# Layer 0 weight split in a float32 decoder trunk: the low part written by ScalarE and an accumulating GpSimd transfer

## The chip, the cores and the metric

The kernel runs on one core of a Trainium2 chip. The metric is the device time of one execution in microseconds. A core has five engines with a queue of their own, each running its instructions in the order in which they stand: TensorE (PE, with its weight loads shown apart as PEld), VectorE (DVE), ScalarE (ACT), GpSimd (POOL) and SyncE (SP), which issues nearly all transfers here.

## The reference

A two-layer decoder trunk over 1024 tokens of width 1024, all in float32. Layer 0 mixes time with RWKV-7 and layer 1 with differential attention; each is followed by a gated convolutional feed-forward part.

```
for l in range(DEPTH):
    h = modulate(rms_norm(x, norm1[l]), sh1, sc1)
    if l < N_A:
        y, v_first = rwkv7_time_mix(h, ...)   # r, k, v = xr @ w_rkv[0], xk @ w_rkv[1], xv @ w_rkv[2]; ... (o * g) @ w_o
    else:
        y = diff_attention(h, k_sh, v_sh, ...)
    x = x + g1 * y
    h2 = modulate(rms_norm(x, norm2[l]), sh2, sc2)
    x = x + g2 * conv_glu_ffn(h2, ...)        # u = h2 @ w_up, a convolution over 3 tokens, silu(gate) * val, @ w_down
return rms_norm(x, final_norm)
```

## The kernel before, in words

A float32 product is made of three float32r products. A weight block W is split into a high part (W rounded to float32r) and a low part (W minus the high part), the activations likewise, and `mm3` (lines 107 to 111) multiplies high by high (L109), low weights by high activations (L110) and high by low (L111), all into one PSUM bank.

In layer 0 the weights of three products go through `mm_cols` (lines 156 to 169). One call makes one block of 128 output columns from pieces of 512 x 128 weights, 256 KB each. For a piece, SP loads it into a `wraw` buffer (L161), ACT rounds it into the high half of a `whl` buffer (L163), an engine that `low()` names subtracts and writes the low half (L164), and PE runs 4 times the three matmuls. With the constants at the end of the file (`LD = 1`, `LN = 0`) `low()` always names DVE. There are 232 pieces: 96 of `a_w_rkv` (48 for each half of the tokens), 48 of `a_w_o` and 88 of `ffn_w_up`. The `wraw` and `whl` buffers are few: 4 and 3 for the first half of `a_w_rkv`, 2 and 2 for its second half and for `a_w_o`, 2 and 4 for `ffn_w_up` (constants `WRB`, `WHB`, `FWR`, `FWH`; `out_proj` asks for 2 and 2).

Five stages use `mm_cols`, in this order:

- A: r, k, v of the first 512 tokens (`tm_proj(0)`), 48 pieces
- B: r, k, v of the other 512 tokens (`tm_proj(1)`), 48 pieces, woven with the recurrence
- C: the output projection of the first 512 tokens in two calls of 256 tokens (`out_proj`), 32 pieces whose matmuls have 256 columns, woven with the recurrence
- D: the feed-forward up product of the first 512 tokens (`ffn_pre`), 88 pieces, woven with the recurrence
- E: the output projection of the last 512 tokens, 16 pieces, alone

The recurrence (`wkv`) goes over eight tiles of 128 tokens, each a chain of small matmuls, DVE and ACT steps; POOL raises to the power -0.5 for it (L581, L307). After stage E the rest of layer 0's feed-forward part and layer 1 do not use `mm_cols`: their weights are split by `split` and `split_w` on ACT and DVE.

`weave`, `merge` and the loop in `trunk` say in which order pieces of work are emitted. A scheduler then places the instructions on each engine's queue; it moves an instruction ahead of others that it does not depend on, so that the rounding of a piece can stand in ACT's queue ahead of work on earlier pieces.

Of the kernel before, what the change touches and what calls it, by code (L numbers as in the profile page):

```python
# [9 lines left out]
F32 = mybir.dt.float32  # L10
F32R = mybir.dt.float32r
BF16 = mybir.dt.bfloat16
AF = mybir.ActivationFunctionType
ALU = mybir.AluOpType
# [3 lines left out]
P = 128  # L18
# [3 lines left out]
HS = 512  # L22
# [63 lines left out]
class Trunk:  # L86
# [69 lines left out]
    def mm_cols(self, ps, w, j, xh, xl, wraw, whl, khs=(0, 1)):  # L156

        nc = self.nc
        for i, kh in enumerate(khs):
            raw = wraw.tile([P, 4, P], F32, tag="wraw", name="wraw")  # L160
            nc.sync.dma_start(raw, w[kh * HS:(kh + 1) * HS, j * P:(j + 1) * P].rearrange("(k p) f -> p k f", p=P))  # L161
            wt = whl.tile([P, 2, 4, P], F32R, tag="whl", name="whl")
            nc.scalar.copy(wt[:, 0], raw)  # L163
            self.low().tensor_tensor(out=wt[:, 1], in0=raw, in1=wt[:, 0].bitcast(F32), op=ALU.subtract)  # L164
            for k in range(4):
                kk = 4 * i + k
                self.mm3(ps, wt[:, 0, k, :], wt[:, 1, k, :], xh[:, kk, :], xl[:, kk, :], kk == 0, kk == 4 * len(khs) - 1)
            if i + 1 < len(khs):
                yield
# [1691 lines left out]
```

## Time and profile before

| | |
|---|---|
| median of 3 runs | 3306.48 us (3298.51 to 3312.58) |
| the profiled execution's own time | 3304.96 us |
| its span on the core | 3303.2 us |
| mean granted TensorE clock | 0.943 of full speed |
| busy: PE, PEld, DVE, ACT, POOL | 91%, 73%, 65%, 37%, 3% of the span |
| stages A to E | about 109 to 1313 us of the span |

The profile is of one execution. A row of the groups by line gives the busy time of all instructions of one line and shape, the mean of one in ns, and the idle time of the engine right before them with what ended it. A timeline row is one instruction with its start and length; in brackets stands how long its engine had been idle and what it had waited for. In the table of windows a time of an engine is its busy time in that stretch, and PEclk is the granted share of the full clock.

### The profile page before, as it was taken

To read this page: it belongs to the slowest core of one execution; us is meant where nothing else is said; L and a number is where in the kernel's file an instruction comes from. 1 tells how busy PE (TensorE), PEld (TensorE's weight loads), DVE (VectorE), ACT (ScalarE), POOL (GpSimd) and SP (SyncE) were. 2 spreads that over 40 slices of the span, in tenths; PEclk is the share of its full clock that TensorE was granted. 3 is DMA by queue.
4 is the path that set the end of the run, shared out by engine and by line. 5 is a ranking of instruction groups with operands and counts; after the bars stand their busy time and mean duration, and the time that the engine had idled before them with its cause. 6 is when DMAs were issued, how large, how long until landed. Compare 5 with 4: busy or idle time off the path is not lost.

```text
span 3303.2 us, 53483 instructions
## 1 busy us (share of the span) xinstructions
PE 3004.2 (91%) x21607; PEld 2419.4 (73%) x21607; DVE 2152.5 (65%) x3752; ACT 1228.2 (37%) x2165; POOL 84.1 (3%) x50
## 2 busy tenths in 40 slices
PE   5988888987899997899999889898889999999997
PEld 2574667776677775788888678787678888888885
DVE  2656778566777855687777676777656655555555
ACT  3634455554454543322223333444333221222123
POOL 0000000000000000000000000000000000000000
PEclk7999899988899998999999899899899999999998
DMA  7363344343433337454443445445552111111111
GB/s 244 113 201 111 98 125 122 115 116 109 117 116 106 100 105 241 153 159 138 141 153 121 149 134 141 136 124 153 151 177 97 52 51 39 58 45 51 39 45 51
DMA packets 441402, 387.85 MB, mean 117 GB/s; under 512 B 42832, under 2 KB 369856, under 8 KB 440130
## 3 DMA queue, kind: packets, MB, share of 16 engines
q1 hardware_dynamic: 438850, 380.23, 38.3%
q8 instruction: 170, 2.79, 0.4%
q10 hardware_dynamic: 2304, 4.20, 0.3%
q14 instruction: 78, 0.64, 0.1%
HBM read 298.74 MB, written 83.49 MB: 116 GB/s over the span
## 4 chain that ended last, share of the span: by engine, by line
PE 68%; DVE 14%; DMA 6%; issue 6%; ACT 4%; POOL 1%; SPq 0%; DVEq 0%; POOLq 0%; ACTq 0%
PE u L109 9%; PE u L110 8%; PE u L111 8%; PE d L109 5%; PE d L111 5%; PE d L110 5%; PE ps L109 5%; PE ps L110 4%; PE ps L111 4%; DMA agw<-in_ada_w_dram 2%; PE wp L696 1%; PE sc L1539 1%; PE cp L745 1%; DVE AS L636 1%; PE tp L1466 1%
## 5 line engine op out<-in xcount | busy, mean ns | idle before, releaser
L109 PE MATMUL u<-h,whl 128*128 128x512 f32 x1408 | 561.8, 399 | 12.7 <-DVE mu L1089 10.0
L110 PE MATMUL u<-h,whl 128*128 128x512 f32 x1408 | 554.3, 394 | 6.2 <-DVE whl L164 6.2
L111 PE MATMUL u<-h,whl 128*128 128x512 f32 x1408 | 552.7, 393 | 0.0
L1134 DVE SCALAR_TENSOR_TENSOR x<-d,mod,x 128x512 f32<-128x512 f32 x352 | 261.8, 749 | 180.7 <-PE d L111 180.6
L109 PEld LDWEIGHTS u<-h,whl 128*128 128x128 f32 x1408 | 265.7, 189 | 73.5 <-ACT h L1090 10.2
L110 PEld LDWEIGHTS u<-h,whl 128*128 128x128 f32 x1408 | 265.8, 189 | 63.3 <-DVE whl L164 8.7
L111 PEld LDWEIGHTS u<-h,whl 128*128 128x128 f32 x1408 | 265.6, 189 | 59.6
L100 ACT CAST whl<-raw 128x1024 fp32r<-128x1024 f32 x140 | 143.9, 1042 | 433.6 <-PE d L111 421.5
L1046 DVE SCALAR_TENSOR_TENSOR a<-u,cwc,a 128x511 f32<-128x511 f32 (+1 forms) x132 | 122.0, 924 | 258.7 <-ACT a L1045 258.6
L109 PE MATMUL d<-hid,whl 128*128 128x512 f32 x704 | 280.1, 398 | 8.3 <-ACT hid L100 6.0
L110 PE MATMUL d<-hid,whl 128*128 128x512 f32 x704 | 277.3, 394 | 0.0
L111 PE MATMUL d<-hid,whl 128*128 128x512 f32 x704 | 275.4, 394 | 0.0
L1045 ACT ACTIVATE a<-u,cwc 128x512 f32<-128x512 f32 (+1 forms) x132 | 121.5, 921 | 390.9 <-PE u L111 390.5
L164 DVE TENSOR_TENSOR whl<-wraw,whl 128x512 fp32r<-128x512 f32 x232 | 158.0, 685 | 123.5 <-ACT whl L163 121.1
L163 ACT CAST whl<-wraw 128x512 fp32r<-128x512 f32 x232 | 142.7, 618 | 248.5 <-PE ps L111 102.9
L109 PE MATMUL ps<-xh,whl 128*128 128x512 f32 x384 | 162.7, 424 | 9.8 <-ACT xh L100 8.2
L101 DVE TENSOR_TENSOR whl<-raw,whl 128x1024 fp32r<-128x1024 f32 x140 | 168.9, 1217 | 4.0 <-ACT whl L100 3.8
L109 PEld LDWEIGHTS d<-hid,whl 128*128 128x128 f32 x704 | 133.2, 189 | 44.4 <-ACT hid L100 9.3
L111 PE MATMUL ps<-xl,whl 128*128 128x512 f32 x384 | 156.7, 409 | 4.6 <-DVE xl L101 4.3
L110 PE MATMUL ps<-xh,whl 128*128 128x512 f32 x384 | 156.4, 408 | 4.4 <-DVE whl L164 4.4
L111 PEld LDWEIGHTS d<-hid,whl 128*128 128x128 f32 x704 | 133.2, 189 | 30.3 <-DVE hid L101 1.6
L110 PEld LDWEIGHTS d<-hid,whl 128*128 128x128 f32 x704 | 133.3, 189 | 26.8
(279 smaller groups left out, 5863.9 us busy)
## 6 DMA issues: line engine op xcount, KB each, us to landing
raw<-in_ffn_w_up_dram SPq DMA_DIRECT2D x88, 512.0 KB
wraw<-in_a_w_rkv_dram SPq DMA_DIRECT2D x96, 256.0 KB
agw<-in_ada_w_dram SPq DMA_DIRECT2D x96, 256.0 KB
wraw<-in_ffn_w_up_dram SPq DMA_DIRECT2D x88, 256.0 KB
raw<-in_ffn_w_down_dram SPq DMA_DIRECT2D x44, 512.0 KB
agw<-in_ada_w_dram SPq DMA_DIRECT2D x128, 128.0 KB
rkv_d<-st SPq DMA_DIRECT2D x48, 256.0 KB
wraw<-in_a_w_o_dram SPq DMA_DIRECT2D x48, 256.0 KB
```

The source lines that it names most:

```text
L100: nc.scalar.copy(h, src)
L101: nc.vector.tensor_tensor(out=l, in0=src, in1=h.bitcast(F32), op=ALU.subtract)
L109: nc.tensor.matmul(ps, wh, xh, start=first, stop=False)
L110: nc.tensor.matmul(ps, wl, xh, start=False, stop=False)
L111: nc.tensor.matmul(ps, wh, xl, start=False, stop=last)
L163: nc.scalar.copy(wt[:, 0], raw)
L164: self.low().tensor_tensor(out=wt[:, 1], in0=raw, in1=wt[:, 0].bitcast(F32), op=ALU.subtract)
L636: nc.vector.tensor_tensor(out=AS[o, hh, :, c, :], in0=Av[o], in1=cst[o, W_AM:W_AM + 64].unsqueeze(1).to_broadcast([64, NK, 64]), op=ALU.mult)
L696: nc.tensor.matmul(Kp[o, j * 64:(j + 1) * 64], T.KB[r, j, c, :], KD[r, hh, c, j, :], start=True, stop=True)
L1045: nc.scalar.activation(a, u, AF.Identity, bias=c[3], scale=c[2])
L1046: nc.vector.scalar_tensor_tensor(out=a[:, 1:], in0=u[:, :n - 1], scalar=c[1], in1=a[:, 1:], op0=ALU.mult, op1=ALU.add)
L1134: nc.vector.scalar_tensor_tensor(out=xs, in0=ps, scalar=gate[:, j:j + 1], in1=xs, op0=ALU.mult, op1=ALU.add)
```

## The change

ACT writes the negated high part into the low half of the `whl` buffer, and a transfer issued by POOL reads the same 256 KB of weights from HBM again and adds them to that half in place. DVE's subtraction is gone. SP's load and ACT's rounding stay.

```diff
         for i, kh in enumerate(khs):
             raw = wraw.tile([P, 4, P], F32, tag="wraw", name="wraw")
-            nc.sync.dma_start(raw, w[kh * HS:(kh + 1) * HS, j * P:(j + 1) * P].rearrange("(k p) f -> p k f", p=P))
+            src = w[kh * HS:(kh + 1) * HS, j * P:(j + 1) * P].rearrange("(k p) f -> p k f", p=P)
+            nc.sync.dma_start(raw, src)
             wt = whl.tile([P, 2, 4, P], F32R, tag="whl", name="whl")
             nc.scalar.copy(wt[:, 0], raw)
-            self.low().tensor_tensor(out=wt[:, 1], in0=raw, in1=wt[:, 0].bitcast(F32), op=ALU.subtract)
+
+            nc.scalar.activation(wt[:, 1], wt[:, 0].bitcast(F32), AF.Copy, scale=-1.0)
+            nc.gpsimd.dma_start(wt[:, 1], src, accum_op=ALU.add)
```

Lines below this place have numbers higher by 3 in the changed kernel. The scheduler's order, at two places. First ACT's queue at the end of stage E (`sq` is the square of an output block, which waits for DVE, and DVE for that block's matmuls; the names in brackets are the semaphores an instruction waits on). Before:

```order
L849 ACTIVATE sq<-xs 128x512 [waits DVE_49,Activation_49]
L163 CAST whl<-wraw 128x512 [waits DMAHW3_49,PE_49,Activation_49]
L163 CAST whl<-wraw 128x512 [waits DMAHW7_49,DVE_49,PE_49]
L849 ACTIVATE sq<-xs 128x512 [waits DVE_49,Activation_49]
L163 CAST whl<-wraw 128x512 [waits DMAHW3_49,PE_49,Activation_49]
L163 CAST whl<-wraw 128x512 [waits DMAHW6_49,DVE_49,PE_49]
L849 ACTIVATE sq<-xs 128x512 [waits DVE_49,Activation_49]
```

With the change:

```order
L852 ACTIVATE sq<-xs 128x512 [waits DVE_49]
L164 CAST whl<-wraw 128x512 [waits DMAHW6_49,DMASW0_49,PE_49]
L166 ACTIVATE whl<-whl 128x512 [waits Activation_49]
L164 CAST whl<-wraw 128x512 [waits DMAHW2_49,DMASW1_49,PE_49]
L166 ACTIVATE whl<-whl 128x512 [waits Activation_49]
L852 ACTIVATE sq<-xs 128x512 [waits DVE_49]
```

Each rounding is followed at once by its negation, no further ahead of the squares than it was; the rounding still waits for PE, whose matmuls free the `whl` buffer.

Second POOL's queue in the recurrence (`inv` and `st` are its powers). Before:

```order
L581 TENSOR_TENSOR inv<-inv,mh 128x8 x4
L307 TENSOR_TENSOR st<-st,mh 128x16
L581 TENSOR_TENSOR inv<-inv,mh 128x8 x2
L307 TENSOR_TENSOR st<-st,mh 128x16
L581 TENSOR_TENSOR inv<-inv,mh 128x8 x2
```

With the change:

```order
L584 TENSOR_TENSOR inv<-inv,mh 128x8
L167 DMA whl<-in_a_w_rkv_dram 128x4x128 x4
L584 TENSOR_TENSOR inv<-inv,mh 128x8
L167 DMA whl<-in_a_w_rkv_dram 128x4x128 x4
L310 TENSOR_TENSOR st<-st,mh 128x16
L167 DMA whl<-in_a_w_rkv_dram 128x4x128 x7
```

The 232 transfers now stand between the powers, which had POOL's queue to themselves.

## Rows read from the trace of the kernel before

**Rows 1.** The page, parts 1 and 4: busy time by engine; the chain that ended last

```profile
PE 3004.2 (91%) x21607; PEld 2419.4 (73%) x21607; DVE 2152.5 (65%) x3752; ACT 1228.2 (37%) x2165; POOL 84.1 (3%) x50
...
PE 68%; DVE 14%; DMA 6%; issue 6%; ACT 4%; POOL 1%; SPq 0%; DVEq 0%; POOLq 0%; ACTq 0%
```

**Rows 2.** Table of windows: stage B, stage D, most of stage E

```profile
330.00:655.00 325.00, 287.66 (x4188) 230.97 (x4185) 227.80 (x491) 172.26 (x348) 18.61 (x8) 0.91 0.38 113
...
850.00:1235.00 385.00, 364.36 (x4392) 293.00 (x4392) 282.57 (x603) 194.96 (x376) 17.66 (x7) 0.97 0.36 107
1265.00:1313.00 48.00, 44.71 (x180) 34.04 (x179) 26.77 (x41) 15.50 (x25) 0.00 (x0) 0.96 0.83 264
```

**Rows 3.** Groups by line: rounding, subtraction, and the low-weight matmuls of three products

```profile
L110 PE MATMUL u<-h,whl 128*128 128x512 f32 x1408 | 554.3, 394 | 6.2 <-DVE whl L164 6.2
...
L164 DVE TENSOR_TENSOR whl<-wraw,whl 128x512 fp32r<-128x512 f32 x232 | 158.0, 685 | 123.5 <-ACT whl L163 121.1 <-DMA wraw<-in_a_w_rkv_dram 1.6
...
L110 PE MATMUL ps<-xh,whl 128*128 128x512 f32 x384 | 156.4, 408 | 4.4 <-DVE whl L164 4.4
...
L163 ACT CAST whl<-wraw 128x512 fp32r<-128x512 f32 x232 | 142.7, 618 | 248.5 <-PE ps L111 102.9 <-DMA wraw<-in_ffn_w_up_dram 80.2 <-DMA wraw<-in_a_w_o_dram 33.1
...
L110 PE MATMUL ps<-oh,whl 128*128 128x512 f32 (+1 forms) x288 | 105.8, 369 | 5.5 <-DVE whl L164 5.4
```

**Rows 4.** Timeline: one piece's load, from SP's issue to ACT's start

```profile
974.95 0.37 SPq L161 DMA_DIRECT2D wraw<-in_ffn_w_up_dram  x1
...
977.96 0.62 ACT L163 CAST whl<-wraw 128x512 fp32r<-128x512 f32 x1 [1.04 <-DMA wraw<-in_ffn_w_up_dram]
```

**Rows 5.** Groups by line: POOL's longest kind of instruction

```profile
L307 POOL TENSOR_TENSOR st<-st,mh 128x16 f32<-128x16 f32 x8 | 24.7, 3088 | 265.9 <-DVE st L306 265.9
```

**Rows 6.** Timeline, stage A: pieces 4, 13 and 25 (from 0)

```profile
125.04 0.19 PEld L110 LDWEIGHTS ps<-xh,whl 128*128 128x128 f32 x1
...
146.30 0.62 ACT L163 CAST whl<-wraw 128x512 fp32r<-128x512 f32 x1 [1.40 <-PE ps L111]
...
152.53 0.19 PEld L110 LDWEIGHTS ps<-xh,whl 128*128 128x128 f32 x1
...
188.09 0.19 PEld L110 LDWEIGHTS ps<-xh,whl 128*128 128x128 f32 x1
```

**Rows 7.** Timeline, stage B: pieces 50, 73 and 95

```profile
361.21 0.79 PE L110 MATMUL ps<-xh,whl 128*128 128x512 f32 x1 [4.39 <-DVE whl L164]
...
504.66 0.63 ACT L163 CAST whl<-wraw 128x512 fp32r<-128x512 f32 x1
...
511.09 0.19 PEld L110 LDWEIGHTS ps<-xh,whl 128*128 128x128 f32 x1
...
651.76 0.19 PEld L110 LDWEIGHTS ps<-xh,whl 128*128 128x128 f32 x1
```

**Rows 8.** Timeline, stage C: pieces 114 and 127

```profile
779.47 0.40 PE L110 MATMUL ps<-oh,whl 128*128 128x256 f32 x2
...
824.85 0.61 ACT L163 CAST whl<-wraw 128x512 fp32r<-128x512 f32 x1
...
826.33 0.19 PEld L110 LDWEIGHTS ps<-oh,whl 128*128 128x128 f32 x1 [0.63 <-DVE whl L164]
```

**Rows 9.** Timeline, stage D: pieces 141 and 187

```profile
900.73 0.62 ACT L163 CAST whl<-wraw 128x512 fp32r<-128x512 f32 x1 [8.31 <-DMA wraw<-in_ffn_w_up_dram]
...
902.12 0.19 PEld L110 LDWEIGHTS u<-h,whl 128*128 128x128 f32 x1 [0.54 <-DVE whl L164]
...
1095.65 0.62 ACT L163 CAST whl<-wraw 128x512 fp32r<-128x512 f32 x1
...
1106.26 0.19 PEld L110 LDWEIGHTS u<-h,whl 128*128 128x128 f32 x1
```

**Rows 10.** Timeline, stage E: pieces 219 and 231

```profile
1273.47 0.19 PEld L110 LDWEIGHTS ps<-oh,whl 128*128 128x128 f32 x1
...
1308.55 0.62 ACT L163 CAST whl<-wraw 128x512 fp32r<-128x512 f32 x1 [2.15 <-DMA wraw<-in_a_w_o_dram]
...
1309.95 0.19 PEld L110 LDWEIGHTS ps<-oh,whl 128*128 128x128 f32 x1 [0.19 <-DVE whl L164]
```

## The prediction

> **What bounds the kernel now.** I read the page first: PE is busy 91% of the span and carries 68% of the chain that ended last; DVE has 14% of the chain, ACT 4%, POOL 1% [rows 1]. So the kernel pays for whatever holds PE. All that changes lies in stages A to E, some 1200 us of 3303. In stage D PE is busy 364 of 385 us, ACT 195, POOL 18 [rows 2]: ACT has room for more work, and PE has almost none for waits. The groups by line then say what the removed step costs: the subtraction takes DVE 685 ns, 232 times, 158.0 us, but PE stood idle for it only 6.2 + 4.4 + 5.5 = 16.1 us in all [rows 3]. Nearly all of DVE's saved time is off the path.
>
> The question is the lead: how long before its low half is wanted does a piece's rounding start? The reader is to take, in the timeline, the start of ACT's L163 and the start of the first low-weight load, PEld L110, of the same piece. The leads are: stage A 152.53 - 146.30 = 6.23 us [rows 6]; B 511.09 - 504.66 = 6.43 [rows 7]; C 826.33 - 824.85 = 1.48 [rows 8]; D 1.39 for one piece and 10.61 for another [rows 9]; E 1309.95 - 1308.55 = 1.40 [rows 10]. Today a piece needs 0.62 (rounding) + 0.69 (subtraction) = 1.31 us.
>
> **What a piece needs after the change.** ACT rounds, 0.62, then negates the same 128 x 512, which I price as the rounding, 0.62 [rows 3]; then POOL writes the transfer's descriptors, the transfer reads 256 KB of weights, reads the half it adds to, writes it, and signals. Call that T. The trace has no transfer from POOL and no adding one. From below: SP's plain load of the same 256 KB reached ACT 977.96 - 974.95 = 3.01 us after its issue [rows 4], so T = 3.0. From above: an instruction of POOL's as long as its longest kind, 3.09 us [rows 5], then two transfers one after the other (weights in, destination read and written back), 6.0: T = 9.1. The adding transfer has parts of all three, overlapped in part; the DMA engines also serve SP's loads, at a share of 0.36 in D and 0.83 in E [rows 2]. I take T = 6.5, a little above the middle. A piece then needs 0.62 + 0.62 + 6.5 = 7.74 us, more than five of the six leads above.
>
> One rule speaks for a longer T. DVE is busy 283 of 385 us in D [rows 2], so nearly every transfer would be made beside a DVE instruction. The Trainium skill (SBUF — State Buffer, section "SBUF: two separate sides") says that GpSimd cannot write descriptors while a DVE instruction of a two-port mode holds their shared port. No row here shows that. If each transfer waited out one DVE instruction of 0.7 us, the sum below would be some 40 us more, about 3520. I don't put it into the sum, since the subtractions and most of DVE's work in these stages have two inputs, and the page names copies and casts.
>
> **Stage by stage.** Two bounds for each. The lower one: a `whl` buffer comes free with its piece's last matmul, and the next piece in it needs 7.74 us and then its own matmuls, so a stage cannot go faster than one piece per (7.74 + matmuls) / buffers. A piece's 12 matmuls are about 3.0 us, the period of stage A where PE never pauses: (188.09 - 125.04) / 21 = 3.00 [rows 6]; with 256 columns I take half, 1.5. The upper one: each piece with a short lead stalls PE by the whole difference, and no stall helps the next.
>
> - A, three buffers: (7.74 + 3.0) / 3 = 3.58 per piece against 3.00, over 21 pieces +12; from above 21 x (7.74 - 6.23) = 32. The row says that L163 waits for PE, the buffer bound at work: **12**. The later pieces have longer leads and add nothing.
> - B, two buffers: 5.37 against (651.76 - 361.21) / 45 = 6.46 [rows 7]: 0; from above 45 x (7.74 - 6.43) = 59. The recurrence's work between the pieces takes up part of a stall, since DVE and ACT go on with it while PE waits: **20**.
> - C, two buffers: (7.74 + 1.5) / 2 = 4.62 against (826.33 - 779.47) / 13 = 3.60 [rows 8], about 28 of 32 pieces being that close: +28; from above 28 x (7.74 - 1.48) = 175. Here PE's queue alternates pieces and recurrence, and a stalled piece delays the recurrence behind it too: **80**, between the two.
> - D, four buffers: 2.69, while the pieces from 141 to 187 come every (1106.26 - 902.12) / 46 = 4.4 us [rows 9]: 0. I count 24 of 88 pieces with leads like the short one; from above 24 x 6.35 = 152. They come in about six runs, and the short one's rounding waited for its load, not for PE, so one stall buys the pieces behind it their lead: 6 x 6.35, **40**.
> - E, two buffers, nothing beside: 5.37 against (1309.95 - 1273.47) / 12 = 3.04 [rows 10], over 14 pieces +33; from above 14 x (7.74 - 1.40) = 89. The DMA engines are at 0.83 here, so T is at its longest: **40**.
>
> Sum +192. From it goes PE's wait for DVE, 16. ACT's 232 x 0.62 = 144 us more I cost at nothing: ACT is busy half of stages B and D [rows 2], and if that cover were gone the copies of the recurrence would be late. DVE's other 142 us I also cost at nothing, hidden by PE. POOL's powers now queue behind transfers that wait for ACT; the recurrence waits for them, but a next tile's front is emitted a whole tile ahead, so again nothing. SP's loads can only start earlier, a `wraw` buffer being free after the rounding and not after the subtraction; the runs of D gain from that, which is in the 40. Where an adding transfer stalls PE, what is late next is the piece behind it in the same two buffers.
>
> Result: 192 - 16 = 176 on the profiled execution's 3304.96, which is 1.5 below the median: **3480 us**, 5.3% slower. With T = 9.1 the same steps give about 45, 70, 150, 80 and 60, some 3695. With T = 4.2 only C and E stall at all, about 25 to 30 less 16, some 3320.
>
> **Rivals.**
>
> *Faster.* If T is about 3.0, as SP's load [rows 4], a piece needs 4.24: A, B and D are covered, C's buffers would allow (4.24 + 1.5) / 2 = 2.87 and E's (4.24 + 3.0) / 2 = 3.62, 8 us lost. Against this stand DVE's 16 us of PE idle, and perhaps 20 more where DVE's subtractions stand in front of the recurrence's steps (the wait of stage B's piece 50 is 4.39 us for one subtraction queued behind other DVE work [rows 7]). 3305 - 36 + 8 = 3277. It decides where T is below about 3.5. For it: leads of 6 us in A and B and 10 in much of D; against it: the leads of 1.4 to 1.5 in C and E, and that three parts in series would have to cost what one does. The Trainium skill (DMA: Bandwidth & Descriptors, section "Anatomy of one DMA — SWDGE (gpsimd) path") would have it so: about 2.0 us plus the bytes at 436 GB/s for a transfer issued from GpSimd, an estimate of 2.6 us for 256 KB; it does not speak of adding there.
>
> *Hidden.* T near 4: 25 lost, 16 regained, within 0.5%, about 3310.
>
> *POOL becomes the bound.* 512 rows of 512 bytes are described by POOL one transfer after another. If it is held for 6 us by each, no stage can go faster than that: A 21 x 3.0 = 63 for the close pieces and some 50 for the others, C 28 x 2.4 = 67 and up to twice that with the recurrence behind it, D 88 x 1.6 = 141, E 42, B 70 from a longer T: about 3840. It decides from 4.4 us per transfer, D's period. For it: POOL takes 3.09 us for a power of 16 numbers per partition [rows 5]; against it: nothing shows its time for a transfer.
>
> That the change doesn't do what it says I rule out: the listing of POOL's queue has the transfers, and DVE's subtraction at L164 is gone.
>
> **How the numbers follow.** About 0.5% is what a measurement of this kernel can tell from no change. The forecast, stalls from a T of 4.5 to 9, has 0.70; POOL bound 0.15; hidden 0.08; faster 0.07. Slower is the forecast and POOL bound, 0.85. The range goes from 3320, the sum at T = 4.2, to 3740, a little over the sum at T = 9.1 and the lower part of POOL bound; outside lie the faster case, much of the hidden one and the worst of POOL.
>
> **What would show it.** POOL's row for L167 and the time from a negation's end to the L110 it releases give T. Right: PE idle before L110 put down to a DMA into `whl`, some 150 to 250 us, most in C, then D and E; C's tight pieces at 4.6 us or more, E's at 5.4; the granted clock in E below 0.96. Wrong: L110 idle of less than 30 us (T short), or POOL busy over 80% in stages A to D (POOL bound), or stalls in C and E alone (the recurrence and the loads took up the others).

## The result and the profile after

The changed kernel takes **3504.26 us** (median of 4 runs, 3502.61 to 3511.08) against 3307.45 (3298.51 to 3312.58, 4 runs) beside it: a ratio of **1.0598 [1.0577, 1.0618]**, 5.98% slower. The forecast was 3480, 5.3% slower, in a range of 3320 to 3740. The profiled execution took 3504.64 us with a span of 3502.9 and a mean granted clock of 0.925 (before 0.943).

The page of the changed kernel, busy time by engine (part 1) and DMA queues (part 3: packets, MB, share of 16 engines' span), answering [rows 1]:

```profile
PE 3073.8 (88%) x21607; PEld 2456.4 (70%) x21607; DVE 2023.3 (58%) x3520; ACT 1360.4 (39%) x2397; POOL 381.7 (11%) x282
...
q1 hardware_dynamic: 438850, 380.23, 36.5%
q0 software_dynamic: 122496, 60.83, 14.1%
```

Two things stand in the first row. DVE's busy time fell by 129 us and ACT's rose by 132, as planned (less than the 158.0 and 145.3 us of the rows by line, because instructions that follow each other overlap a little in the record). But PE, with the same 21607 matmuls, is busy 69.6 us longer than the 3004.2 of [rows 1]. The queue q0 is POOL's: it moves 61 MB in 14.1% of the DMA engines' time, SP's q1 380 MB in 36.5%.

The groups by line of the changed kernel, answering [rows 3] (busy us, mean ns, then the idle time right before with what ended it):

```profile
L110 PE MATMUL u<-h,whl 128*128 128x512 f32 x1408 | 555.5, 395 | 9.1 <-DMA whl<-in_ffn_w_up_dram 9.1
...
L110 PE MATMUL ps<-xh,whl 128*128 128x512 f32 x384 | 170.5, 445 | 57.5 <-DMA whl<-in_a_w_rkv_dram 57.4
...
L166 ACT ACTIVATE whl<-whl 128x512 fp32r<-128x512 f32 x232 | 145.3, 629 | 4.7
...
L164 ACT CAST whl<-wraw 128x512 fp32r<-128x512 f32 x232 | 142.4, 618 | 276.9 <-PE ps L111 216.3 <-PE u L111 30.8 <-DMA wraw<-in_ffn_w_up_dram 22.4
...
L167 POOL DMA_DIRECT2D whl<-in_a_w_rkv_dram x96 | 125.1, 1326 | 428.2 <-ACT whl L166 384.2 <-PE ps L111 11.1 <-PE cp L726 8.8
...
L110 PE MATMUL ps<-oh,whl 128*128 128x512 f32 (+1 forms) x288 | 119.8, 417 | 64.5 <-DMA whl<-in_a_w_o_dram 64.5
```

At the low-weight matmuls PE now waits for the adding transfers: 9.1 + 57.4 + 64.5 = 131.0 us, where it waited 16.1 for DVE. Of the 199.7 us by which the span grew, 115 are this wait (131 less 16) and 70 are a slower PE; the other 15 are other waits. Where that happens, the table of windows says, cut at the ends of the five stages (the last matmul of each stage's pieces). Before:

```profile
109.00:278.00 169.00, 156.44 (x715) 126.50 (x716) 97.16 (x171) 77.69 (x134) 0.00 (x0) 0.95 0.57 175
278.00:655.00 377.00, 331.84 (x4356) 248.49 (x4356) 265.57 (x564) 199.28 (x397) 22.98 (x12) 0.91 0.37 108
655.00:828.00 173.00, 137.35 (x2426) 123.58 (x2422) 118.31 (x267) 90.14 (x204) 11.99 (x5) 0.86 0.40 116
828.00:1235.00 407.00, 379.78 (x4676) 306.47 (x4676) 297.24 (x627) 207.25 (x399) 20.64 (x9) 0.96 0.36 107
1235.00:1313.00 78.00, 58.16 (x232) 44.66 (x232) 42.01 (x62) 26.92 (x46) 2.89 (x1) 0.85 0.80 253
```

With the change (the columns are again the stretch and its length, then PE, PEld, DVE, ACT and POOL busy, PEclk, DMA share, GB/s):

```profile
109.00:321.00 212.00, 172.95 (x716) 134.09 (x716) 68.19 (x121) 104.20 (x181) 60.70 (x47) 0.88 0.93 196
321.00:745.00 424.00, 352.39 (x4340) 256.60 (x4340) 242.43 (x521) 225.40 (x442) 81.52 (x58) 0.88 0.57 125
745.00:967.00 222.00, 158.67 (x2519) 140.95 (x2518) 100.84 (x236) 110.68 (x240) 55.11 (x38) 0.82 0.63 128
967.00:1376.00 409.00, 374.77 (x4593) 300.22 (x4592) 247.99 (x535) 254.58 (x482) 131.05 (x96) 0.95 0.83 163
1376.00:1510.00 134.00, 77.85 (x232) 55.65 (x232) 33.24 (x47) 36.60 (x62) 23.60 (x17) 0.72 0.72 178
```

The reader is to compare, row by row, the length, PE's busy time and PEclk. In us, with the idle time before L110 of the same stretches and the forecast's terms:

| stage | forecast | growth (ends in the trace) | idle at L110 for transfers | PE busy longer |
|---|---|---|---|---|
| A | 12 | 43 | 16 | 17 |
| B | 20 | 48 | 41 | 21 |
| C | 80 | 49 | 34 | 21 |
| D | 40 | 2 | 9 | -5 |
| E | 40 | 55 | 31 | 20 |
| sum | 192 | 197 | 131 | 73 |

The last two columns make up the growth of C and E to within 6 us. In B they are 14 more than it: other waits of PE got shorter. In A they are 10 less; what fills that is shown below. Stage D, with four buffers, loses nothing. One thing blurs the line between C and D: with the change 93 more of PE's matmuls fall into C's stretch and 83 fewer into D's, work of the recurrence that has moved. The pieces' own matmuls alone, whose number stays the same, took 14, 21, 12, 5 and 20 us longer in A to E; about 10 us of C's growth is moved work. (The forecast's 16 us for DVE's waits are inside the growth here, so the sum to set beside 197 is 176.)

What the transfer itself takes is in the view of line L167 (duration of POOL's instruction, min/median/max ns; then issue to landing):

```profile
L167 POOL DMA_DIRECT2D whl<-in_a_w_rkv_dram x96: 1282/1282/1880, 71.0 to 736.5; - x96
...
DMA to landing us min/median/max: 4.2/5.7/11.7
```

And one turn of the two buffers in stage E, from the timeline of the changed kernel:

```profile
1430.00 0.79 PE L110 MATMUL ps<-oh,whl 128*128 128x512 f32 x1 [3.83 <-DMA whl<-in_a_w_o_dram]
...
1434.01 0.63 PE L110 MATMUL ps<-oh,whl 128*128 128x512 f32 x1
...
1435.10 0.62 ACT L164 CAST whl<-wraw 128x512 fp32r<-128x512 f32 x1 [8.30 <-PE ps L111]
...
1435.77 0.39 PE L110 MATMUL ps<-oh,whl 128*128 128x512 f32 x1
...
1436.68 1.29 POOL L167 DMA_DIRECT2D whl<-in_a_w_o_dram  x1 [8.72 <-ACT whl L166]
...
1443.26 0.79 PE L110 MATMUL ps<-oh,whl 128*128 128x512 f32 x1 [4.30 <-DMA whl<-in_a_w_o_dram]
...
1504.31 0.80 PE L110 MATMUL ps<-oh,whl 128*128 128x512 f32 x1 [4.04 <-DMA whl<-in_a_w_o_dram]
```

PE waits 3.83 us, starts the piece, and the piece's last matmul lets ACT round into the buffer at 1435.10. POOL starts the transfer at 1436.68, it is there at 1443.26, and PE has again waited 4.30. So the lead this piece needs is 8.16 us, T is 6.58, and two pieces take 13.26 us. Over pieces 219 to 231 it is (1504.31 - 1430.00) / 12 = 6.19 per piece, where [rows 10] gave 3.04. The matmuls' lengths show the second loss: 0.63 us at first, 0.39 later. The table of windows for the two parts of that turn:

```profile
1430.00:1434.80 4.80, 4.80 (x11) 3.76 (x12) 0.00 (x0) 0.00 (x0) 0.00 (x0) 0.50 1.15 283
1435.60:1438.00 2.40, 2.37 (x11) 1.63 (x9) 2.27 (x4) 1.50 (x4) 1.29 (x1) 1.00 0.46 131
```

After standing idle for 3.83 us PE was granted 0.50 of its clock, the 1.2 GHz level, and ran 11 matmuls in 4.80 us; then 1.00, the 2.4 GHz level, and 11 in 2.37. The wait is paid, and then part of it once more.

### The profile page after: what moved, and what is told of

Same layout as the page of the kernel before. It is cut to its first block, busy times and chain, and to the rows that moved or that the text cites. A ratio compares the mean times of both kernels' runs of the same rounds, so it can differ in the third digit from the quotient of the medians.

```text
span 3502.9 us, 53886 instructions
## 1 busy us (share of the span) xinstructions
PE 3073.8 (88%) x21607; PEld 2456.4 (70%) x21607; DVE 2023.3 (58%) x3520; ACT 1360.4 (39%) x2397; POOL 381.7 (11%) x282
## 3 DMA queue, kind: packets, MB, share of 16 engines
q1 hardware_dynamic: 438850, 380.23, 36.5%
q0 software_dynamic: 122496, 60.83, 14.1%
## 4 chain that ended last, share of the span: by engine, by line
PE 59%; DVE 9%; DMA 8%; issue 5%; ACT 3%; POOL 1%; SPq 0%; DVEq 0%; POOLq 0%; ACTq 0%
PE u L109 8%; PE u L110 8%; PE u L111 8%; PE d L109 5%; PE d L111 5%; PE d L110 5%; PE ps L110 4%; PE ps L109 4%; PE ps L111 4%; DMA whl<-in_a_w_o_dram 3%; DMA whl<-in_a_w_rkv_dram 1%; DMA agw<-in_ada_w_dram 1%; PE wp L699 1%; PE sc L1542 1%; PE tp L1469 1%
## 5 line engine op out<-in xcount | busy, mean ns | idle before, releaser
L109 PE MATMUL u<-h,whl 128*128 128x512 f32 x1408 | 564.6, 401 | 11.3 <-DVE mu L1092 9.8
L110 PE MATMUL u<-h,whl 128*128 128x512 f32 x1408 | 555.5, 395 | 9.1 <-DMA whl<-in_ffn_w_up_dram 9.1
L109 PEld LDWEIGHTS u<-h,whl 128*128 128x128 f32 x1408 | 266.9, 190 | 71.6 <-ACT h L1093 10.1
L110 PEld LDWEIGHTS u<-h,whl 128*128 128x128 f32 x1408 | 267.1, 190 | 66.3 <-DMA whl<-in_ffn_w_up_dram 11.9
L109 PE MATMUL d<-hid,whl 128*128 128x512 f32 x704 | 282.1, 401 | 7.9 <-ACT hid L100 6.0
L110 PE MATMUL d<-hid,whl 128*128 128x512 f32 x704 | 278.8, 396 | 0.0
L164 ACT CAST whl<-wraw 128x512 fp32r<-128x512 f32 x232 | 142.4, 618 | 276.9 <-PE ps L111 216.3
L110 PE MATMUL ps<-xh,whl 128*128 128x512 f32 x384 | 170.5, 445 | 57.5 <-DMA whl<-in_a_w_rkv_dram 57.4
L286 DVE SCALAR_TENSOR_TENSOR agacc<-agw,dv,agacc 128x256 f32<-128x256 f32 (+1 forms) x196 | 116.9, 596 | 136.7 <-DMA agw<-in_ada_w_dram 134.6
L109 PE MATMUL ps<-xh,whl 128*128 128x512 f32 x384 | 173.3, 452 | 13.4 <-ACT xh L100 9.0
L110 PE MATMUL ps<-oh,whl 128*128 128x512 f32 (+1 forms) x288 | 119.8, 417 | 64.5 <-DMA whl<-in_a_w_o_dram 64.5
L167 POOL DMA_DIRECT2D whl<-in_a_w_rkv_dram x96 | 125.1, 1326 | 428.2 <-ACT whl L166 384.2
L111 PE MATMUL ps<-xl,whl 128*128 128x512 f32 x384 | 167.1, 436 | 3.2 <-DVE xl L101 3.0
L109 PEld LDWEIGHTS d<-hid,whl 128*128 128x128 f32 x704 | 134.3, 191 | 44.0 <-ACT hid L100 9.6
```

The costliest lines, as they stand in the source:

```text
L109: nc.tensor.matmul(ps, wh, xh, start=first, stop=False)
L110: nc.tensor.matmul(ps, wl, xh, start=False, stop=False)
L111: nc.tensor.matmul(ps, wh, xl, start=False, stop=last)
L167: nc.gpsimd.dma_start(wt[:, 1], src, accum_op=ALU.add)
L286: nc.vector.scalar_tensor_tensor(out=acc, in0=w, scalar=self.ca[:, k:k + 1], in1=acc, op0=ALU.mult, op1=ALU.add)
```

## The experiments

The theories were: **latency** (each piece needs rounding, negation and T, and where two or three buffers give a shorter lead PE waits, and then runs slowly); **ACT** (its 144 us more delay other work); **traffic** (232 transfers of 256 KB more on the DMA engines delay other loads). Growth by stage is read as above, one trace against the trace of the kernel before; in only_D, only_E and only_A below, the stages that were left alone differ from it by up to 3 us, so less than that says nothing.

### ACT's part alone: DVE adds in place of the transfer (neg_dve)

```diff
-            nc.gpsimd.dma_start(wt[:, 1], src, accum_op=ALU.add)
+            nc.vector.tensor_tensor(out=wt[:, 1], in0=raw, in1=wt[:, 1].bitcast(F32), op=ALU.add)
```

> ScalarE's negation is kept, and VectorE adds the weights to it in place of the transfer: no work of GpSimd, no second read of the weights. Latency theory (the loss is TensorE waiting for the adding transfer): a piece needs 0.62 + 0.63 + 0.69 = 1.94 us instead of 1.31, so only stages C and E, with leads near 1.4 us, lose something: 3305 to 3330 us. Rival 'ScalarE is the bound' (the second pass of 0.63 us delays the recurrence's copies): a good part of the 197 us, over 3380 us.

3318.65 us, 1.0049 [1.0032, 1.0066], as expected, though A and not C or E grew most: the stages A to E grew by 6, 4, 1, 2 and 3 us. ACT ran all its 232 negations: 145 us more on ACT, 0.63 us longer per piece, cost some 15 us in this trial, not nothing as forecast. ACT's row of the rounding (groups by line) is wanted later, for stage D:

```profile
L164 ACT CAST whl<-wraw 128x512 fp32r<-128x512 f32 x232 | 142.5, 617 | 210.4 <-PE ps L111 80.1 <-DMA wraw<-in_ffn_w_up_dram 74.1 <-DMA wraw<-in_a_w_o_dram 25.8
```

### The transfer beside the path (aside_ACDE, aside4_ACE)

In the named stages DVE subtracts as before, and ACT also negates and POOL also adds, but into a tile `scr` that nobody reads. Same traffic, same POOL, no wait of PE for it.

```diff
+            if stage in "ACDE":
+                self.low().tensor_tensor(out=wt[:, 1], in0=raw, in1=wt[:, 0].bitcast(F32), op=ALU.subtract)
+                scr = wraw.tile([P, 4, P], F32R, tag="scr", name="scr")
+                nc.scalar.activation(scr, wt[:, 0].bitcast(F32), AF.Copy, scale=-1.0)
+                nc.gpsimd.dma_start(scr, src, accum_op=ALU.add)
...
```

> In stages A, C, D and E VectorE subtracts as before, and the negation and the adding transfer are made as well, into a buffer that nobody reads; stage B is as before. Latency theory: TensorE does not wait for these transfers, so what is left is ScalarE's, GpSimd's and the queues' work: 3310 to 3350 us. Rival 'traffic' (61 MB more, and GpSimd's queue, slow the other transfers and the recurrence): most of what stages A, C, D and E lost, about 3307 + 100 to 150 = 3400 to 3450 us.

3402.7 us, 1.0305 [1.0276, 1.0335], far above what the latency theory gave and inside the traffic rival's 3400 to 3450. A grew by 33 us, B (as before the change) by 1, C 12, D 41, E 15. D's part is the trial's own doing, ACT waiting for one of only two `scr` buffers (groups by line):

```profile
L169 ACT ACTIVATE scr<-whl 128x512 fp32r<-128x512 f32 x184 | 115.4, 630 | 84.7 <-DMA scr<-in_ffn_w_up_dram 48.7 <-DMA scr<-in_a_w_o_dram 33.3
```

Stage A had four `scr` buffers and no such wait. So the second trial has four in A, C and E and leaves D as before:

> As the run with the unread transfers, but with four buffers for them, so that ScalarE does not wait for a transfer before its next negation, and in stages A, C and E alone. What TensorE loses here cannot be its wait for a low half. Stage A should lose 30 us again (its loads share the DMA engines with the transfers), C and E under 10 us each if the 12 and 15 us of the other run came from ScalarE's waits for a buffer: 3335 to 3350 us. If C and E lose as before, 3360 us: then transfers cost there by their traffic too.

3377.69 us, 1.0223 [1.0203, 1.0242]: more than either figure expected. A grew by 29, B by 2, C 15, D 5, E 16. By the sign set beforehand (C and E lose as before, 12 and 15 there), the transfers cost something by their traffic in C and E too. ACT's row of the rounding says how:

```profile
L164 ACT CAST whl<-wraw 128x512 fp32r<-128x512 f32 x232 | 142.3, 617 | 252.6 <-PE ps L111 96.7 <-DMA wraw<-in_ffn_w_up_dram 80.7 <-DMA wraw<-in_a_w_o_dram 50.4
```

ACT waits 50.4 us for SP's loads of `a_w_o`, the weights of C and E, where it waited 33.1 [rows 3]; for those of D, left alone, it waits as before. PE's idle time at the high-weight matmuls (L109) for the rounding rose from 1.7 to 9.5 us in C and from 1.4 to 5.3 in E. In the changed kernel `wraw` comes free sooner, and the part is small there: with leads enough, C and E lose 4 and 5 us (late_buf below).

In A, the groups by line of its own stretch (108 to 307 us):

```profile
L110 PE MATMUL ps<-xh,whl 128*128 128x512 f32 x192 | 78.0, 408 | 0.0
...
L298 PE MATMUL agps<-cst,agacc 128*128 128x1 f32 x28 | 5.3, 294 | 29.4 <-DVE agacc L291 29.4
```

PE never waits at L110, and yet A is 29 longer. It waits 29.4 us for `agacc`, the modulation vectors, which DVE sums from weights that SP loads (`agw`). Before:

```profile
L290 PE MATMUL agps<-cst,agacc 128*128 128x1 f32 x28 | 4.4, 261 | 7.6 <-DVE agacc L283 7.6
```

and in the changed kernel, in its stage A:

```profile
L293 PE MATMUL agps<-cst,agacc 128*128 128x1 f32 x28 | 5.3, 294 | 16.5 <-DVE agacc L286 16.5
```

DVE's own wait for those weights, before (190 to 278 us) and in the trial (200 to 311 us):

```profile
DVE agacc L283 <- DMA agw<-in_ada_w_dram: 28.7, 24, 2.9
...
DVE agacc L291 <- DMA agw<-in_ada_w_dram: 50.9, 29, 7.0
```

ACT's negations alone do not do this: with them, neg_dve's stage A grew by 6 us and PE waited 9.4 for `agacc`. The traffic theory holds in A. The DMA queues there, as shares of 16 engines, in the second half of stage A before (190 to 278 us):

```profile
q1 hardware_dynamic: 23048, 16.55, 61.3%
```

and with the change (205 to 321 us):

```profile
q1 hardware_dynamic: 24606, 17.63, 51.2%
q0 software_dynamic: 13206, 6.56, 45.9%
```

Before, the packets of SP's transfers took 0.613 x 88 = 54 us, counted over 16 engines. With the change SP's take 0.512 x 116 = 59 and the adding ones 0.459 x 116 = 53 (25 transfers, 528 packets and 2.1 us each): 112 of 116 us. That does not show that the engines were full: the times of packets overlap, and the share can pass 1, as the 1.15 of 1430 to 1434.8 us above. It shows that the packet time of this stretch doubled. What remained of A's growth in the table, 10 us, is mostly PE's longer wait for the modulation, 16.5 against 7.6.

### More buffers (buf62_6)

```diff
-WHB = (3, 2)
+WHB = (6, 2)
-                self.pool("wraw", 2, side) as wraw, self.pool("whl", 2, side) as whl:
+                self.pool("wraw", 2, side) as wraw, self.pool("whl", 6, side) as whl:
```

> The changed kernel with more buffers for the split weights: 6 instead of 3 in stage A, 6 instead of 2 in C and E; B (2, no room) and D (4) as they are. Latency theory: with six buffers a piece may be begun 5 pieces ahead, 5 x 3 us or more, over the 7 us that it needs; stages A, C and E lose most of their 42 + 49 + 55 us: 3380 to 3430 us. Rivals 'ScalarE' and 'traffic': more buffers take away neither, 3490 to 3510 us.

3422.67 us, 1.036 [1.0336, 1.0385]. C's growth fell from 49 to 14 us, E's from 55 to 7, A's from 43 to 28 (with 7 more ahead of A); B, which kept two buffers, grew by 53, D by 13. The groups by line:

```profile
L110 PE MATMUL ps<-xh,whl 128*128 128x512 f32 x384 | 166.9, 435 | 43.7 <-DMA whl<-in_a_w_rkv_dram 43.7
...
L110 PE MATMUL ps<-oh,whl 128*128 128x512 f32 (+1 forms) x288 | 108.8, 378 | 24.9 <-DMA whl<-in_a_w_o_dram 24.9
```

Most of the loss of C and E, 83 of 104 us, was the lead, set by the number of buffers; 14 and 7 us stay. The mean of the `oh` matmuls (stages C and E among them) also fell, from 417 to 378 ns: fewer waits, fewer slow matmuls.

### The transfer without its adding (plain_pool)

POOL copies 256 KB of zeros from HBM, in rows of 512 bytes, over the low half. The source is one array, filled at the start and read again for every piece.

```diff
-            nc.gpsimd.dma_start(wt[:, 1], src, accum_op=ALU.add)
+            nc.gpsimd.dma_start(wt[:, 1].bitcast(F32), self.dum)
```

> GpSimd's transfer copies instead of adding, from an array of zeros in HBM with rows of the same 512 bytes (the low parts of layer 0's weights are left out). If the adding is what makes the transfer long, its landing falls from 5.7 us to near 4 and the kernel to about 3400 us. If GpSimd's writing of the descriptors and the fixed part make it, landing stays above 5.2 us and the kernel at 3480 to 3510 us.

3424.84 us, 1.0368 [1.0332, 1.0403]; A to E grew by 24, 28, 38, -7 and 42. From its page (POOL's queue, part 3; POOL's instruction, part 5; the issues with their median us to landing, part 6):

```profile
q0 software_dynamic: 18560, 60.83, 6.1%
...
L167 POOL DMA_DIRECT2D whl<-dum_d x232 | 175.6, 757 | 991.1 <-ACT whl L166 777.4
...
whl<-dum_d POOLq DMA_DIRECT2D x232, 256.0 KB, 4.2
```

Adding is 1.5 us of T (5.7 against 4.2), 0.5 us of POOL's time, 528 packets for 80, and over twice the DMA time (14.1% against 6.1%). It makes 79 us of the loss (3504 - 3425), if the one source read again and again made no difference. The rest is there with a plain copy: 0.62 + 0.63 + 4.2 = 5.5 us is still longer than the short leads in C and E. The rival *faster* wanted a T below about 3.5, and neither 5.7 nor 4.2 is that. The Trainium skill (DMA: Bandwidth & Descriptors, section "Anatomy of one DMA — SWDGE (gpsimd) path") has a fit of about 2.0 us plus the bytes at 436 GB/s, from which an estimate of 2.6 us for 256 KB follows; the trace does not agree, 4.2 us for the plain copy, and the measurement decides.

### Wanting the low half later (late_after, late_before)

Each piece's eight matmuls with the high part first, the four with the low part last (L174 in the runs).

```diff
             for k in range(4):
-                self.mm3(ps, wt[:, 0, k, :], wt[:, 1, k, :], xh[:, kk, :], xl[:, kk, :], ...)
+                nc.tensor.matmul(ps, wt[:, 0, k, :], xh[:, kk, :], ...)
+                nc.tensor.matmul(ps, wt[:, 0, k, :], xl[:, kk, :], ...)
+            for k in range(4):
+                nc.tensor.matmul(ps, wt[:, 1, k, :], xh[:, kk, :], ...)
```

> The changed kernel, with each piece's matmuls in another order: first the four with high weights and both activations (8 matmuls), then the four with the low weights. Nothing of the transfers, ScalarE or GpSimd changes; a low half is wanted 7 matmuls of about 0.23 us later, 1.6 us. Latency theory: each of some 65 stalls becomes up to 1.6 us shorter, and with it goes part of the slow matmuls after stalls: 3504 - 60 to 110 = 3390 to 3440 us. Traffic theory: no change, 3490 to 3510 us.

3457.77 us, 1.0462 [1.044, 1.0484]: 46 us back, less than expected. Growth A to E 38, 35, 40, 7, 33. The groups by line:

```profile
L174 PE MATMUL ps<-xh,whl 128*128 128x512 f32 x384 | 120.2, 439 | 41.6 <-DMA whl<-in_a_w_rkv_dram 41.6
...
L174 PE MATMUL ps<-oh,whl 128*128 128x256 f32 (+1 forms) x192 | 50.8, 395 | 52.0 <-DMA whl<-in_a_w_o_dram 52.0
```

Eight matmuls now stand ahead of the wait where one did. The seven more take 7/12 of 3.0 us and add only some 1.75 us to a lead that in E lacked 8.16 - 1.40.

> The kernel before with the same order of matmuls. TensorE stood idle 16 us for VectorE's subtraction; most of that should go: 3288 to 3303 us, faster by 0.1 to 0.5%. If the idle time only moves to the next wait, 3303 to 3308 us.

On the kernel before the same order gives 3306.75, 1.0003 [0.9989, 1.0017]: no gain, as expected if the 16 us of idle time only move to the next wait.

### One stage alone (only_D, only_E, only_A)

The new path where `stage in "D"`, `"E"` or `"A"`, DVE's subtraction elsewhere.

> The new path in stage D alone (88 of 232 pieces); the other stages are the kernel before. Stage D was 2 us longer with the change although its adding transfers land in 6.0 us. Latency theory: four buffers and leads near 11 us hide them: 3300 to 3320 us. Traffic theory: 23 MB of adding transfers slow D's loads: 3330 us or more. If VectorE's freed 60 us are worth something in the recurrence: under 3295 us.

3302.89 us, 0.9997 [0.9982, 1.0011]. In D, L110's wait for DVE became one of the same size for the transfer:

```profile
L110 PE MATMUL u<-h,whl 128*128 128x512 f32 x1408 | 555.6, 395 | 6.3 <-DMA whl<-in_ffn_w_up_dram 6.3
```

Four buffers hide 88 transfers whole, and DVE's 60 us less (88 x 0.685), with ACT's 55 more beside them, buy nothing.

> The new path in stage E alone (16 of 232 pieces); the other stages subtract on DVE as before. Theory that E's loss is made in E by two buffers and the wait for the adding transfer: E grows by 45 to 55 us as it did in the whole change, its granted clock falls to about 0.75, the time is 3350 to 3358. Rival that part of E's loss is carried over from the stages before it (late loads, late recurrence): E grows by 30 us or less, 3335 or less.

3358.77 us, 1.0161 [1.0143, 1.0179]. E grew by 55, no other stage by more than 3. The whole of E's loss is made in E, by 16 transfers:

```profile
L110 PE MATMUL ps<-oh,whl 128*128 128x512 f32 (+1 forms) x288 | 112.4, 392 | 34.2 <-DMA whl<-in_a_w_o_dram 32.0 <-DVE whl L170 2.2
```

> The new path in stage A alone (48 pieces). Theory that A loses by its own traffic (late loads of the other weights and clock) beside a short wait at the low-weight matmul: A grows by about 40 us, 3340 to 3347. Rival that the 43 us of A in the whole change are partly work that only moved from A to B (loads for later stages started earlier): A grows by 40 but the whole time by 20 or less, 3325 or less.

3341.44 us, 1.0104 [1.0089, 1.0119]. A grew by 38 and the time by 35: A's loss stays, it isn't moved to B. In its stage A, the groups by line:

```profile
L110 PE MATMUL ps<-xh,whl 128*128 128x512 f32 x192 | 81.8, 427 | 15.8 <-DMA whl<-in_a_w_rkv_dram 15.6
...
L296 PE MATMUL agps<-cst,agacc 128*128 128x1 f32 x28 | 5.2, 291 | 14.2 <-DVE agacc L289 14.2
```

### Buffers and late matmuls together (late_buf)

> The whole change with six buffers for the split weights in the first half of r, k, v and in the output projection, and each piece's four low-weight matmuls last. Theory that waits and what the clock loses behind them make the loss in C and E and half of A, and traffic the rest of A: PE's idle time for the transfers at the low-weight matmuls falls under 40 us (79 with the buffers alone), the time to 3385 to 3405, and A still loses 20 to 30. Rival that traffic makes most of the rest: 3415 to 3425, as with the buffers alone.

3403.24 us, 1.0292 [1.0275, 1.0309], inside the time expected. Growth A to E 32, 34, 4, 8, 5, and 8 ahead of A. The waits left, over the whole span, are 48 us and not under 40, most of them in B with its two buffers:

```profile
L174 PE MATMUL ps<-xh,whl 128*128 128x512 f32 x384 | 116.8, 429 | 33.8 <-DMA whl<-in_a_w_rkv_dram 33.8
...
L174 PE MATMUL u<-h,whl 128*128 128x512 f32 x352 | 98.5, 402 | 6.1 <-DMA whl<-in_ffn_w_up_dram 6.1
...
L174 PE MATMUL ps<-oh,whl 128*128 128x256 f32 (+1 forms) x192 | 41.9, 341 | 8.1 <-DMA whl<-in_a_w_o_dram 8.1
```

In its stage A alone (108 to 319 us):

```profile
L174 PE MATMUL ps<-xh,whl 128*128 128x512 f32 x192 | 54.0, 405 | 0.2 <-DMA whl<-in_a_w_rkv_dram 0.2
L297 PE MATMUL agps<-cst,agacc 128*128 128x1 f32 x28 | 5.3, 292 | 30.8 <-DVE agacc L290 30.8
```

This run tells the two causes apart. With leads enough, C and E lose 4 and 5 us. A still loses 32 with no wait at the low-weight matmuls (0.2 us): 23 of them (30.8 - 7.6) are the modulation's late weights. Take the wait at L110 away in A, and the same time is lost one wait later.

No version made here beats the kernel before.

## Why the prediction was right, and where it was not

- **The mechanism held.** "Needs 7.74 us, more than five of the six leads": T is 5.7 in the median and 6.58 in the turn of E shown (6.5 was taken); the leads were too short, and PE waits at L110 for the transfer. More buffers (buf62_6) remove most of the loss where they were added in C and E.
- **The sum came out by compensation, which is luck.** 192 us of stalls were forecast, 131 measured. What filled the gap is PE's slower clock behind the stalls, 70 us of busy time, a term that the sum didn't have. It was forecast only as a sign to look for ("the granted clock in E below 0.96": 0.72 over the whole stage, where it was 0.85). With this second loss a stall of 4 us had to be priced at some 6 to 7: in E, 31 us of waiting and 20 of slower PE. The Trainium skill (TensorE: Matmul & The Clock Gate, section "HAM oscillation — how this bites in real kernels") tells of such a case, a matmul loop in which a DMA wait between its steps throttles PE, so that every next step starts at the lower clock. The windows 1430 to 1438 agree, 0.50 then 1.00.
- **Stage A, 12 forecast, 43 measured.** The failed step is that the traffic was counted only in T. It also delays other loads: the modulation's weights, 9 us of A in the changed kernel, 22 and 23 where the wait at L110 was taken away. The rest of the 43 is 16 us of waiting at L110 and 17 of slower PE. The packet time before, 54 us of 88, plus 25 transfers at 2.1 us, is 107 us and more than the stretch: a warning, though no proof, and the price of 2.1 us wasn't to be had from the trace before.
- **Stage B, 20 forecast, 48 measured.** The buffer bound gave 0 there (5.37 against a mean period of 6.46) and the term was a guess between 0 and 59. PE idles 41 us at L110. A mean period hides that pieces come in close runs between steps of the recurrence: before, the first L110 matmuls of neighbouring pieces of B stood 2.7 to 19.7 us apart. That B's loss is its two buffers is argued, from its waits at L110 and from those left in late_buf; a third buffer in B, or unread transfers there, were not tried.
- **Stage C, 80 forecast, 49 measured.** The lower bound was good: pieces 114 to 127 come every 5.2 us, as in the timeline of the changed kernel (forecast 4.62, "4.6 or more"):

```profile
897.89 0.28 PE L110 MATMUL ps<-oh,whl 128*128 128x256 f32 x1
...
965.50 0.39 PE L110 MATMUL ps<-oh,whl 128*128 128x256 f32 x1
```

  (965.50 - 897.89) / 13 = 5.2. The addition for a delayed recurrence was too much. Of the 49 us, about 10 are recurrence work that stood in D before.
- **Stage D, 40 forecast, 2 measured, 0 alone.** The failed step is "about six runs", each paying one stall of 6.35 us: the leads before were taken as fixed. Taken from the starts of the 88 roundings and of their pieces' first L110 load, 23 of them were under 7.5 us before (the shortest 1.4), and one with the change (7.1). The short roundings had waited for their loads, and these now come sooner, `wraw` being free after the rounding: ACT's wait for `ffn_w_up` fell from the 80.2 us of [rows 3] to 22.4 in the row of L164 above. The runs show that this is the cause: where DVE still reads `wraw`, in neg_dve, the wait stays at 74.1 us and 24 leads are under 7.5; in only_D, where it doesn't, the wait is 25.6 and one lead is. The forecast named this gain, and then charged six stalls all the same.
- **Stage E, 40 forecast, 55 measured.** Waiting is 31, as the lower bound's 33. The forecast's turn of 5.37 per piece took the piece's matmuls at 3.0 us; after the stall they take about 5.1 (1430.00 to ACT's release at 1435.10), in every second piece, so 6.19.
- **ACT's extra pass at nothing:** 15 us in the neg_dve trial. **DVE's saved time at nothing:** right (only_D). **POOL as the bound:** refuted, 1.28 us per transfer and 11% busy, against 4.4 from which it decides. (That rival's terms add up to 433 to 500 us, some 3740 to 3805, and not to the 3840 it names.)
- **The rule on the shared port:** POOL's instruction has a median equal to its minimum, 1282 ns, with DVE busy 58% of the span. 34 of the 232 took longer than 1.32 us, four of them with no DVE instruction beside. So the length of the instruction shows no such wait as a rule; whether some of the time to landing is one, no run here tells.
- **The signs:** idle at L110 "150 to 250 us, most in C, then D and E" was 131, most in B, then C and E. The pieces in C came at 5.2 us, as their sign said (4.6 or more), those in E slower than theirs (6.19 against 5.4).

Left open: by what means the added transfers delay SP's loads. With plain copies in plain_pool A still grew by 24 us, though there those copies took less than half of the adding ones' packet time.

## What to carry to other kernels

Before an engine's step is replaced by a transfer, compare the lead that the buffers give (time from the buffer's release to its first reader) with the whole chain of the transfer; where it was shorter, PE paid the difference here and then part of it again in a lower clock, and DVE, which was off the path, gave nothing back. Ask also which loads gain, because a buffer comes free sooner, and which lose: add the packet time of the new transfers to that of each stretch. Where they came to about the stretch's length, in A, other loads were late, and removing the first wait only uncovered theirs. Check a forecast stage by stage, since a right total can be made of wrong terms.

## What the runs showed of the hardware

- A transfer from POOL that adds 256 KB into SBUF, in rows of 512 bytes: 5.7 us to landing (4.2 to 11.7), 1.28 us of POOL, 528 packets, whose times come to 2.1 us counted over 16 engines. Without adding: 4.2 us, 0.76 us, 80 packets, 6.1% against 14.1% of the engines' span for the same 232. Packets of the two queues overlap in time: the share reached 1.15 in E.
- In stage A's second half the packets of SP's queue and of the adding transfers took nearly the same time, 51% to 46%, though SP's moved 2.7 times the bytes.
- Unread adding transfers, on which nothing waits, made ACT's waits for SP's loads of `a_w_o` 50.4 us where they were 33.1, and DVE's for `agw` in A's second half 50.9 of 111 us where they were 28.7 of 88.
- The stalls of 3.8 to 4.9 us in stage E, five of them, are each followed by a stretch at 0.50 of the clock (in the one shown 4.80 us with 11 matmuls, against 2.40 for 11 at 1.00).
